# A two-layer decoder trunk on one core: VectorE's top-k in written order, four more tiles split on GpSimd, one weight load earlier

## The chip, the core and the metric

One Trainium2 chip, one of its cores. The metric is the device time of one execution in microseconds (us), median of the runs; lower is better. Engines: PE (TensorE matmul; PEld is its weight load), DVE (VectorE), ACT (ScalarE), POOL (GpSimd), SP (the queue that issues most DMAs).

## What is computed

Two layers over 256 tokens of width 1024. Each layer mixes the tokens (a gated linear recurrence beside sparse attention) and then runs an expert-retrieval mixer. The change lies almost wholly in the second half, which is, per layer:

```
q  = x @ wq                                  # 8 heads, 2 x 128 each
s  = einsum('thcd,ckd->thck', q, subkeys)    # two lists of 128 scores per head
sv, si = top_k(s, 16)
cand   = sv[:, :, 0, :, None] + sv[:, :, 1, None, :]
cv, ci = top_k(cand, 16)                     # 16 experts of 16384 per head
experts = ea * 128 + eb                      # ea, eb read from si at ci
gate    = softmax(cv)
y = sum over experts of  gelu(x . u_tab[e]) * gate * v_tab[e]
x = layer_norm(ALPHA * x + y)
```

## The kernel before

The expert tables are not gathered. All 128 tiles of `u_tab` (128 experts each) are multiplied with x, then weighted by a gate that is zero for unchosen experts, then all tiles of `v_tab` are multiplied. So TensorE has a fixed amount of dense work per layer, and the top-k (VectorE) runs beside the first half of it.

**A tile.** `wtile` loads 128x1024 numbers of 4 bytes by DMA into `raw`. ScalarE rounds them to `hi` (L103), and VectorE or GpSimd forms `lo = raw - hi` (L104). TensorE then does 24 matmuls per tile (`col_mm`, L112: 8 chunks, each as hi*hi, lo of x * hi, hi * lo of the weight). There are 4 buffers of `raw`, 3 of `hi`, 3 of `lo`, taken in the order of the tiles: the `hi` and `lo` of a tile can be written only when TensorE is done with the tile three places ahead.

**The top-k zone.** `query(h)` makes the query of head h: heads 4 to 7 need two tiles of `wq` each, whose `lo` is VectorE's. `top(h)` multiplies it with the subkeys (L798, 8 short matmul records), ScalarE copies the scores out of PSUM into `ss` (L800, two buffers), and `best16` finds the 16 best of each of four lists of 128 in five VectorE instructions: the best 8 (MAX8), their places (FIND_INDEX8), a copy without them (MATCH_REPLACE8), the next 8, their places (L785 to L789). FIND_INDEX8 and MATCH_REPLACE8 each have a short MATCH_VALUE_LOAD in front. `pairs(g)` adds the lists of four heads (L812, L816, nine instructions into `cd`) and runs eight `best16` over 50 candidates; `choices(g)` decodes the indices; `turn_round` transposes the result. Heads 2, 0, 1, 3 come first, then `pairs(0)`, heads 4 to 7, `pairs(1)`, `choices`.

**What sets the order.** `work()` is a generator that yields a cost after each piece; the loop below it emits tiles of `u_tab` whenever the costs have used up the `room`. The `lo` of tiles 0 to NPOOL-1 (14) goes to GpSimd. The emitted order isn't the order of an engine: the framework's scheduler reorders each engine's instructions. VectorE waits for its own earlier result through a semaphore.

**Layer 1's start.** `ORDER[1]` lists the steps of the mixing half; `d0` to `d5` are loads of constants, `d1` the weights `lw` of the recurrence's gates (L670), which the matmuls of L370 read.

Of the kernel before, what the change touches and what calls it, by code (L numbers as in the profile page):

```python
# [20 lines left out]
D = 1024  # L21
S = 256
# [24 lines left out]
NHF = 2  # L47
ROOT_ACT = {1, 2, 3}
NACT = 4
NPOOL = 14  # L50
NLATE = 4
NCAND = 50
CNT = [16 // (i + 1) for i in range(16)]
# [24 lines left out]
def trunk_kernel(ctx: ExitStack, tc: tile.TileContext, x, xt, cst, lam, pvec, brow, w_in, w_lx, w_v, w_q4, lru_w,  # L78
# [13 lines left out]
    def bank():  # L92
        return psp.tile([128, 512], F32, tag="ps", name="ps")


    def wtile(src, shape, lo_eng, dst=None):
        n = int(np.prod(shape))
        raw = ring.tile([128, 1024], F32, tag="raw", name="raw", bufs=4)
        if dst is None:
            dst = (ring.tile([128, 1024], F32R, tag="hi", name="hi"), ring.tile([128, 1024], F32R, tag="lo", name="lo"))  # L100
        nc.sync.dma_start(raw[:, :n], src)
        hi, lo, raw = dst[0][:, :n], dst[1][:, :n], raw[:, :n]
        ACT.copy(hi, raw)  # L103
        lo_eng.tensor_tensor(lo, raw, hi, op=ALU.subtract)  # L104
        if len(shape) == 2:
            hi = hi.rearrange("p (a b) -> p a b", a=shape[0])
            lo = lo.rearrange("p (a b) -> p a b", a=shape[0])
        return hi, lo
# [5 lines left out]
    def col_mm(ps, w, xT, t=ALL):  # L114
        for c in range(NCH):
            mm3(ps, (w[0][:, c, :], w[1][:, c, :]), (xT[0][:, c, t], xT[1][:, c, t]), c == 0, c == NCH - 1)
# [13 lines left out]
    def rtile(src, shape):  # L130
        raw = ring.tile([128, 1024], F32, tag="raw", name="raw", bufs=4)
        raw = raw[:, :shape[0] * shape[1]].rearrange("p (a b) -> p a b", a=shape[0])
        nc.sync.dma_start(raw, src)
        return raw
# [91 lines left out]
    for c0, c1 in ((0, 1), (1, 2), (2, 4), (4, 6), (6, 8)):  # L226
        s = slice(c0, c1)
        nc.sync.dma_start(xTf[:, s], xt[:, s])
        w = rtile(w_lx[0, :, s], (c1 - c0, 512))
# [36 lines left out]
    for l in range(NL):  # L266
# [3 lines left out]
        with tc.tile_pool(name="mix", bufs=1, reuse_waits="tile") as mp, \  # L270
# [433 lines left out]
            if l == 0:  # L704
                nc.sync.dma_start(lm, lam)
                psv = [bank(), bank()]
                for c0, c1 in ((0, 3), (3, 6), (6, 8)):
                    w = rtile(w_v[l, :, c0:c1], (c1 - c0, 280))
# [19 lines left out]
        with tc.tile_pool(name="peer", bufs=1, reuse_waits="tile") as pp:  # L728
# [7 lines left out]
            def act_tile():  # L736
                return pp.tile([128, 2, S], F32, name="act", bufs=NACT)

            def u_tile(a):
                if a % 2 == 0:  # L740
                    ub[a] = bank()
                ps = ub[a - a % 2]
                col_mm(ps[:, HALF[a % 2]], wtile(u_tab[l, a], (8, 128), POOL if a < NPOOL else DVE), xT)
                if a % 2:
                    at = act_tile()
                    ACT.activation(at.rearrange("p a b -> p (a b)"), ps, AF.Gelu_apprx_tanh)  # L746
                    kept[a - 1] = spill.tile([128, 2, S], F32, name="kept%d" % (a - 1), bufs=1)
                    ACT.dma_start(kept[a - 1], at)

            with tc.tile_pool(name="topk", bufs=1, reuse_waits="tile") as tk:  # L750
# [17 lines left out]
                def query(h):  # L768
                    qh = tk.tile([128, 2, S], F32, name="qh", bufs=2)
                    if h < 2:  # L770
                        for tb in range(2):
                            ACT.copy(qh[:, :, TB[tb]], qT4[tb][:, 2 * h:2 * h + 2])
                    else:
                        ps = bank()
                        for c in range(2):
                            k = 2 * h + c - 4
                            if "w%d" % k in W:
                                raw_mm(ps[:, c * 256:c * 256 + 256], W["w%d" % k])
                            else:
                                col_mm(ps[:, c * 256:c * 256 + 256], wtile(wq[l, k], (8, 128), POOL if h < 4 else DVE), xT)  # L780
                        ACT.copy(qh.rearrange("p a b -> p (a b)"), ps)
                    qhs[h] = qh

                def best16(v, ix, src, tmp):
                    DVE.max(v[:, 0:8], src)  # L785
                    DVE.max_index(ix[:, 0:8], v[:, 0:8], src)  # L786
                    DVE.match_replace(tmp, v[:, 0:8], src, -3e38)  # L787
                    DVE.max(v[:, 8:16], tmp)
                    DVE.max_index(ix[:, 8:16], v[:, 8:16], tmp)  # L789

                def top(h):

                    qh = qhs.pop(h)
                    ps = bank()
                    for tb in range(2):
                        for c in range(2):
                            k = tb * 2 + c
                            PE.matmul(ps[:, k * 128:k * 128 + 128], qh[:, c, TB[tb]], skt[:, c], start=True, stop=True)  # L798
                    ss = tk.tile([128, 4, 128], F32, name="ss", bufs=2)
                    ACT.copy(ss.rearrange("p a b -> p (a b)"), ps)  # L800
                    s2 = tk.tile([128, 4, 128], F32, name="s2", bufs=2)
                    for tb in range(2):
                        for c in range(2):
                            k, j = tb * 2 + c, tb * 4 + h % 4
                            best16(sv[:, h // 4, j, c], si[:, h // 4, j, c], ss[:, k], s2[:, k])
                            yield 1.45

                def pairs(g):

                    a, b = sv[:, g, :, 0], sv[:, g, :, 1]  # L810
                    for i in range(8):
                        DVE.tensor_tensor(cd[:, :, OFF[i]:OFF[i] + CNT[i]], a[:, :, i:i + 1].to_broadcast([128, 8, CNT[i]]),  # L812
                                          b[:, :, :CNT[i]], op=ALU.add)
                        if i % 4 == 3:
                            yield 1.2
                    DVE.tensor_tensor(cd[:, :, OFF[8]:NCAND], a[:, :, 8:16],  # L816
                                      b[:, :, 0:1].to_broadcast([128, 8, 8]), op=ALU.add)
                    for j in range(8):
                        best16(cv[:, g, j], ci[:, g, j], cd[:, j], c2[:, j])
                        yield 1.05  # L820
# [55 lines left out]
                    yield 1.8  # L876

                def turn_round():
                    for w in range(3):
                        ps = bank()  # L880
                        for tb in range(2):
                            src = ev[:, w, tb] if w < 2 else gate[:, tb]
                            PE.transpose(ps[:, TB[tb]], src.rearrange("p g k -> p (g k)"), ident)
                        tok = ps[:, :256].rearrange("p (q i) -> p q i", i=2)
                        if w < 2:
                            DVE.tensor_copy(eT[:, :, w], tok)
                        else:
                            DVE.tensor_scalar(gT[:, :, 0], tok, GSC, None, op0=ALU.mult)
                            DVE.scalar_tensor_tensor(gT[:, :, 1], tok, GSC, gT[:, :, 0], op0=ALU.mult, op1=ALU.subtract)
                        yield 0.5  # L890

                def work():
                    for h in (2, 0, 1, 3):
                        yield from top(h)
                    yield from pairs(0)
                    query(4)
                    yield 2.44 - 5.76
                    for h in range(4, 8):
                        if h < 7:
                            query(h + 1)  # L900
                            yield 2.44 - 5.76
                        yield from top(h)
                    yield from pairs(1)
                    yield from choices(0)
                    yield from choices(1)
                    yield 1.0
                    yield from turn_round()
                    yield 4.0

                for h in (2, 0, 1, 3):  # L910
                    if h == 0:
                        q_rows(1)
                    query(h)
                a, room = 0, 0.0
                for cost in work():
                    room -= cost
                    while room < 0 and a < 96:
                        u_tile(a)
                        room += 2.88 if a < NPOOL else 1.66
                        a += 1  # L920

            with tc.tile_pool(name="dense", bufs=1, reuse_waits="tile") as dp:

# [145 lines left out]
                for j, p in enumerate(body):  # L1069
# [11 lines left out]
                    if left <= 14 and pre:  # L1081
                        f, i = pre.pop(0)
                        f(i)
                        if left <= len(pre):
                            f, i = pre.pop(0)
# [194 lines left out]
```

## Time and profile before

| | us |
|---|---|
| three runs | 1940.72, 1940.97, 1942.93; median 1940.97 |
| the profiled execution, its own time | 1938.31 |
| its span, first to last instruction | 1936.5 |
| mean granted TensorE clock | 0.991 of full |

The span is what the views divide; 1.8 us of the execution lie around it, and the profiled execution is 2.7 us under the median. Times in the views count from the span's start. In layer 0 the top-k zone lies at about 160 to 340 us, in layer 1 at about 1124 to 1304. A busy PE isn't PE at its peak: starts of matmuls per microsecond tell more than the busy share.

### The profile page before, as it was taken

What the parts mean: (1) busy time and instruction counts of PE and PEld (TensorE: products, weight loads), DVE (VectorE), ACT (ScalarE), POOL (GpSimd) and SP (SyncE); (2) the same over time, 40 slices, a digit from 0 to 9 for tenths busy, and PEclk for the clock granted to TensorE, in tenths of its full rate; (3) what the DMA queues carried; (4) which work ended last, traced back from release to release, by engine and by line L of the source; (5) the groups of instructions that cost most, each with busy time, mean ns of one, the idle gap of its engine ahead of it and who ended that gap; (6) DMA issues with size and microseconds to landing.
All of it is one profiled execution on the core that took longest, in us unless ns stands there. A gap on an engine that the chain in (4) does not pass through costs nothing.

```text
span 1936.5 us, 32461 instructions
## 1 busy us (share of the span) xinstructions
PE 1894.0 (98%) x12580; PEld 1679.2 (87%) x12580; DVE 1330.6 (69%) x2553; ACT 966.3 (50%) x1579; POOL 83.1 (4%) x55
## 2 busy tenths in 40 slices
PE   8999899999999999999999998999999999999998
PEld 7858899999999888888777498999999998888886
DVE  5763994766666776767657549946666656777776
ACT  3635444555555555556445344444555555555553
POOL 0005200000000000000000062000000000000000
PEclk9999999999999999999999999999999999999999
DMA  7505557666667777888362054576666677778783
GB/s 267 175 1 172 153 191 236 211 207 192 204 203 242 244 241 240 282 283 300 140 227 66 0 187 154 189 236 212 196 203 201 201 245 240 244 243 286 250 265 106
DMA packets 130095, 393.91 MB, mean 203 GB/s; under 512 B 15634, under 2 KB 16404, under 8 KB 129812
## 3 DMA queue, kind: packets, MB, share of 16 engines
q1 hardware_dynamic: 111508, 358.28, 57.8%
q10 hardware_dynamic: 18432, 33.56, 4.7%
q8 instruction: 98, 1.61, 0.3%
q14 instruction: 57, 0.47, 0.1%
HBM read 357.18 MB, written 34.60 MB: 202 GB/s over the span
## 4 chain that ended last, share of the span: by engine, by line
PE 88%; DVE 8%; DMA 2%; issue 1%; ACT 1%; SPq 0%; POOL 0%; DVEq 0%; ACTq 0%; POOLq 0%
PE ps L112 39%; PE ps L995 34%; PE ps L954 3%; PE ps L119 3%; PE ps L590 3%; DVE lo L104 1%; PE ps L562 1%; DMA raw<-in_v_tab_dram 1%; PE ps L515 1%; DVE si L789 1%; DVE cd L812 1%; PE ps L232 1%; DVE s L787 1%; DVE si L786 0%; DVE t L866 0%
## 5 line engine op out<-in xcount | busy, mean ns | idle before, releaser
L104 DVE TENSOR_TENSOR lo<-raw,hi 128x1024 fp32r<-128x1024 f32 x516 | 635.1, 1232 | 396.4 <-ACT hi L103 396.0
L103 ACT CAST hi<-raw 128x1024 fp32r<-128x1024 f32 x548 | 575.1, 1050 | 663.4 <-PE ps L112 412.0
L112 PE MATMUL ps<-xThi,lo 128*128 128x256 f32 x2400 | 685.4, 286 | 20.0 <-DVE lo L104 19.7
L112 PE MATMUL ps<-xThi,hi 128*128 128x256 f32 x2400 | 693.5, 289 | 0.0
L112 PE MATMUL ps<-xTlo,hi 128*128 128x256 f32 x2400 | 684.0, 285 | 0.0
L995 PE MATMUL ps<-hi,W 128*128 128x512 f32 x1936 | 517.8, 389 | 0.0
L112 PEld LDWEIGHTS ps<-xThi,lo 128*128 128x128 f32 x2400 | 465.4, 194 | 21.9 <-DVE lo L104 21.2
L112 PEld LDWEIGHTS ps<-xThi,hi 128*128 128x128 f32 x2400 | 465.7, 194 | 0.9 <-issue 0.4
L112 PEld LDWEIGHTS ps<-xTlo,hi 128*128 128x128 f32 x2400 | 465.8, 194 | 0.3
L995 PEld LDWEIGHTS ps<-hi,W 128*128 128x128 f32 x1936 | 363.2, 188 | 75.4
L995 PE MATMUL ps<-lo,W 128*128 128x512 f32 x968 | 298.1, 389 | 0.2 <-DVE lo L104 0.2
L995 PEld LDWEIGHTS ps<-lo,W 128*128 128x128 f32 x968 | 181.6, 188 | 38.2 <-DVE lo L104 0.6
L986 ACT CAST W<-act 128x256 fp32r<-128x256 f32 x242 | 96.1, 402 | 94.6 <-PE ps L995 90.4
L987 DVE TENSOR_TENSOR W<-act,W 128x256 fp32r<-128x256 f32 x242 | 100.0, 422 | 9.5
L104 POOL TENSOR_TENSOR lo<-raw,hi 128x1024 fp32r<-128x1024 f32 x32 | 79.6, 2493 | 355.9 <-ACT hi L103 355.6
L972 DVE TENSOR_TENSOR act<-act,G 128x512 f32<-128x512 f32 x128 | 87.5, 685 | 6.6 <-DMA act<-kept 6.6
L958 ACT ACTIVATE G<-ps 128x256 f32<-128x256 f32 x256 | 81.2, 383 | 5.3
L943 DVE TENSOR_TENSOR ohg<-ohg,gT 128x2048 f16<-128x2048 f16 x64 | 78.2, 1225 | 2.0
L939 DVE TENSOR_TENSOR ohg<-iota,eT 128x2048 f16<-128x2048 f16 x64 | 77.9, 1220 | 0.0
L746 ACT ACTIVATE act<-ps 128x512 f32<-128x512 f32 x128 | 75.7, 591 | 0.1
L954 PE MATMUL ps<-ohg 128*128 128x128 f16 x1024 | 69.9, 219 | 0.0
L954 PEld LDWEIGHTS <-ohg 128*128 128x128 f16 x1024 | 58.8, 97 | 2.8
(256 smaller groups left out, 1179.6 us busy)
## 6 DMA issues: line engine op xcount, KB each, us to landing
raw<-in_u_tab_dram SPq DMA_DIRECT2D x256, 512.0 KB, 3.6
raw<-in_v_tab_dram SPq DMA_DIRECT2D x256, 512.0 KB, 4.2
kept<-act ACTq DMA_DIRECT2D x128, 256.0 KB, 2.5
act<-kept SPq DMA_DIRECT2D x128, 256.0 KB, 4.1
raw<-in_w_in_dram SPq DMA_DIRECT2D x24, 512.0 KB, 4.5
raw<-in_wq_dram SPq DMA_DIRECT2D x24, 512.0 KB, 3.6
ow<-in_w_out_dram SPq DMA_DIRECT2D x16, 512.0 KB, 7.8
qf<-in_w_q_dram SPq DMA_DIRECT2D x8, 512.0 KB, 3.8
```

Of the source, the lines that this page charges most:

```text
L103: ACT.copy(hi, raw)
L104: lo_eng.tensor_tensor(lo, raw, hi, op=ALU.subtract)
L112: PE.matmul(ps, a[m], b[n], start=start and i == 0, stop=stop and i == 2)
L746: ACT.activation(at.rearrange("p a b -> p (a b)"), ps, AF.Gelu_apprx_tanh)
L939: DVE.tensor_tensor(oh.rearrange("p q w a i -> p (q w) a i"), iota.unsqueeze(1).to_broadcast([128, 8, 128, 2]), eT[:, qs].rearrange("p q w ...
L943: DVE.tensor_tensor(og, oh[:, :, 0:1].to_broadcast([128, 4, 2, 128, 2]), gT[:, qs].unsqueeze(3).to_broadcast([128, 4, 2, 128, 2]), op=ALU. ...
L954: PE.matmul(ps[:, k * 128:k * 128 + 128], oh[:, q, 1, :, i], og[:, q, w, :, i], start=w == 0, stop=w == 1)
L958: ACT.activation(G[g][:, :, t1:t1 + 4], ps.rearrange("p (t g a) -> p g a t", g=2, a=64)[:, g], AF.Copy, scale=1.0 / GSC)
L972: i = DVE.tensor_tensor(act[a0], act[a0], G[a0 // 64][:, a0 % 64:a0 % 64 + 2, :], op=ALU.mult)
L986: ACT.copy(whi, at[:, a % 2])
L987: DVE.tensor_tensor(wlo, at[:, a % 2], whi, op=ALU.subtract)
L995: PE.matmul(accs[tb * 2 + hf], ww[m][:, TB[tb]], v[n][:, hf * 512:hf * 512 + 512], start=a == first[0] and (m, n) == (0, 0), stop=a == 127 ...
```

## The change

Five edits in the top-k zone and one in layer 1's list of steps:

- VectorE's instructions of the zone keep the order in which they are written (`manual_schedule`); the other engines are scheduled as before.
- `scores_of(h)` is taken out of `top(h)` and called ahead of the lists that need it; `query(4)` comes ahead of `top(3)`, and each later query ahead of the lists of the head before.
- NPOOL is 18 and not 14: four more `lo` per layer on GpSimd.
- The budget starts at -6.0 (two tiles more are written ahead of the first lists), and a tile of VectorE's counts 1.55 and not 1.66.
- `turn_round` does its three transposes first, then lets tiles pass, then copies.
- In layer 1, `d1` stands right behind `d0`.

```diff
-         "c0 I1 I0 d0 d4 P c1 V0 d2 V2 V1 d3 V3 d1 G0 d5 G3 G1 T g1 b0 g0 b1 g2 h0 g3 G2 q2 h1 D S q3 q1 kv q0 "
+         "c0 I1 I0 d0 d1 d4 P c1 V0 d2 V2 V1 d3 V3 G0 d5 G3 G1 T g1 b0 g0 b1 g2 h0 g3 G2 q2 h1 D S q3 q1 kv q0 "
...
-NPOOL = 14
+NPOOL = 18
...
-                def top(h):
-
+                sss = {}
+
+                def scores_of(h):
                     qh = qhs.pop(h)
...
+                    sss[h] = ss
+
+                def top(h, k0=0, k1=4):
+
+                    ss = sss[h]
                     s2 = tk.tile([128, 4, 128], F32, name="s2", bufs=2)
-                    for tb in range(2):
+                    for tb in range(k0 // 2, k1 // 2):
...
                 def work():
-                    for h in (2, 0, 1, 3):
-                        yield from top(h)
-                    yield from pairs(0)
+                    scores_of(2)
+                    scores_of(0)
+                    yield from top(2)
+                    scores_of(1)
+                    yield from top(0)
+                    scores_of(3)
+                    yield from top(1)
                     query(4)
                     yield 2.44 - 5.76
+                    yield from top(3)
+                    yield from pairs(0)
+                    scores_of(4)
                     for h in range(4, 8):
                         if h < 7:
                             query(h + 1)
                             yield 2.44 - 5.76
-                        yield from top(h)
+                        yield from top(h, 0, 2)
+                        if h < 7:
+                            scores_of(h + 1)
+                        yield from top(h, 2, 4)
                     yield from pairs(1)
                     yield from choices(0)
                     yield from choices(1)
-                    yield 1.0
                     yield from turn_round()
                     yield 4.0
...
-                a, room = 0, 0.0
-                for cost in work():
-                    room -= cost
-                    while room < 0 and a < 96:
-                        u_tile(a)
-                        room += 2.88 if a < NPOOL else 1.66
-                        a += 1
+                a, room = 0, -6.0
+                with tc.manual_schedule(engines={mybir.EngineType.DVE}):
+                    for cost in work():
+                        room -= cost
+                        while room < 0 and a < 96:
+                            u_tile(a)
+                            room += 2.88 if a < NPOOL else 1.55
+                            a += 1
```

Where the instructions move. First VectorE at the first lists of layer 0; `sv` are values, `si` places, `s_1471` the copy without the best eight. Before:

```order
L785 MAX sv<-ss 128x8 x2
L786 MAX_INDEX si<-sv,ss 128x8
L787 MATCH_REPLACE s_1471<-sv,ss 128x128
L786 MAX_INDEX si<-sv,ss 128x8
L788 MAX sv<-s_1471 128x8
L787 MATCH_REPLACE s_1471<-sv,ss 128x128
L789 MAX_INDEX si<-sv,s_1471 128x8
```

Now:

```order
L785 MAX sv<-ss 128x8
L786 MAX_INDEX si<-sv,ss 128x8
L787 MATCH_REPLACE s_1480<-sv,ss 128x128
L788 MAX sv<-s_1480 128x8
L789 MAX_INDEX si<-sv,s_1480 128x8
L785 MAX sv<-ss 128x8
L786 MAX_INDEX si<-sv,ss 128x8
```

Before, two lists alternate; now a list is finished before the next begins, and each instruction but MATCH_REPLACE and the first MAX reads what the one in front wrote.

Second, SP's loads of layer 0's zone, the order in which tiles pass through the buffers. Before:

```order
L752 DMA skt<-in_sk_dram 128x256
L101 DMA raw<-in_wq_dram 128x1024 x2
L101 DMA raw<-in_u_tab_dram 128x1024 x12
L101 DMA raw<-in_wq_dram 128x1024 x6
L101 DMA raw<-in_u_tab_dram 128x1024
L101 DMA raw<-in_wq_dram 128x1024 x2
L101 DMA raw<-in_u_tab_dram 128x1024 x115
```

Now:

```order
L101 DMA raw<-in_wq_dram 128x1024 x2
L101 DMA raw<-in_u_tab_dram 128x1024 x9
L101 DMA raw<-in_wq_dram 128x1024 x2
L101 DMA raw<-in_u_tab_dram 128x1024 x4
L101 DMA raw<-in_wq_dram 128x1024 x2
L101 DMA raw<-in_u_tab_dram 128x1024
L101 DMA raw<-in_wq_dram 128x1024 x2
L101 DMA raw<-in_u_tab_dram 128x1024
L101 DMA raw<-in_wq_dram 128x1024 x2
L101 DMA raw<-in_u_tab_dram 128x1024 x113
```

The six query tiles that came in one row behind u-tile 11 now come in pairs: behind u-tiles 8, 12, 13 and 14. With NPOOL at 18, all u-tiles up to 17 are GpSimd's.

Third, VectorE around the second pair of query tiles (`lo` of `query(5)`), behind the last list of `pairs(0)`. Now:

```order
L785 MAX cv<-cd 128x8
L786 MAX_INDEX ci<-cv,cd 128x8
L787 MATCH_REPLACE c_1366<-cv,cd 128x50
L788 MAX cv<-c_1366 128x8
L789 MAX_INDEX ci<-cv,c_1366 128x8
L104 TENSOR_TENSOR lo<-raw,hi 128x1024 x2
L785 MAX sv<-ss 128x8
```

All of `pairs(0)` stands between the `lo` of `query(4)` and these two; the four lists of head 3 stand ahead of `pairs(0)`.

## Rows read from the trace of the kernel before

**Rows 1.** The page's first part: busy time by engine

```profile
PE 1894.0 (98%) x12580; PEld 1679.2 (87%) x12580; DVE 1330.6 (69%) x2553; ACT 966.3 (50%) x1579; POOL 83.1 (4%) x55
```

**Rows 2.** Busy time in a stretch: us, PE, PEld, DVE, ACT, POOL, clock, DMA

```profile
200.00:262.00 62.00, 53.11 (x416) 52.50 (x415) 61.97 (x252) 25.59 (x32) 8.79 (x3) 0.94 0.47 145
```

**Rows 3.** The chain that ended last, both zones and layer 1's start: start, us, what

```profile
170.52 8.63 PE ps L112 x72
...
192.44 0.91 PE ps L798 x8
...
340.54 0.66 PE ps L883 x6
...
358.47 0.94 PE ps L954 x16
...
990.39 6.86 DMA lw<-in_lru_w_dram
...
1156.19 0.91 PE ps L798 x8
...
1323.37 0.94 PE ps L954 x16
```

**Rows 4.** Busy time by stretches of 4 us, layer 0, columns as in rows 2

```profile
208.00:212.00 4.00, 1.31 (x6) 1.31 (x7) 3.97 (x25) 0.62 (x2) 0.00 (x0) 0.82 0.09 11
212.00:216.00 4.00, 4.00 (x28) 4.00 (x28) 4.00 (x4) 3.55 (x4) 0.00 (x0) 0.76 0.45 141
```

**Rows 5.** VectorE in order of time: start, us, instruction, out<-in

```profile
187.35 0.49 DVE L785 MAX8 sv<-ss 128x8 f32<-128x128 f32 x2 [1.12 <-ACT ss L800]
...
191.12 0.29 DVE L789 FIND_INDEX8 si<-sv,s 128x8 uint32<-128x128 f32 x1
191.33 0.08 DVE L787 MATCH_VALUE_LOAD s<-sv,ss 128x8 f32 x1
191.38 0.28 DVE L787 MATCH_REPLACE8 s<-sv,ss 128x128 f32<-128x128 f32 x1
191.70 0.30 DVE L788 MAX8 sv<-s 128x8 f32<-128x128 f32 x1
192.03 0.09 DVE L789 MATCH_VALUE_LOAD si<-sv,s 128x8 f32 x1
```

**Rows 6.** VectorE by line: the same MAX8 over 50 candidates; busy, mean ns, idle

```profile
L788 DVE MAX8 cv<-c 128x8 f32<-128x50 f32 x32 | 6.6, 207 | 0.0
```

**Rows 7.** VectorE and GpSimd in order of time, where both add or subtract

```profile
200.18 2.40 POOL L104 TENSOR_TENSOR lo<-raw,hi 128x1024 fp32r<-128x1024 f32 x1 [0.48 <-ACT hi L103]
200.30 2.88 DVE L812 TENSOR_TENSOR cd<-sv 128x128 f32<-128x128 f32 x6
...
235.15 3.54 POOL L104 TENSOR_TENSOR lo<-raw,hi 128x1024 fp32r<-128x1024 f32 x1 [7.55 <-ACT hi L103]
...
236.55 3.22 DVE L104 TENSOR_TENSOR lo<-raw,hi 128x1024 fp32r<-128x1024 f32 x1
...
259.35 0.73 DVE L812 TENSOR_TENSOR cd<-sv 128x128 f32<-128x128 f32 x6
...
261.26 1.23 DVE L104 TENSOR_TENSOR lo<-raw,hi 128x1024 fp32r<-128x1024 f32 x1
```

**Rows 8.** ScalarE in order of time, layer 0's zone; idle time and releaser in brackets

```profile
171.14 0.61 ACT L800 COPY ss<-ps 128x512 f32<-128x512 f32 x1
...
186.73 0.59 ACT L800 COPY ss<-ps 128x512 f32<-128x512 f32 x1
...
196.17 1.05 ACT L103 CAST hi<-raw 128x1024 fp32r<-128x1024 f32 x1 [2.21 <-PE ps L112]
```

**Rows 9.** SP's queue, VectorE and PE in order of time, layer 1's start

```profile
987.90 0.48 SPq L674 DMA_DIRECT2D cw<-in_cmp_w_dram  x1
...
996.87 2.36 DVE L104 TENSOR_TENSOR lo<-raw,hi 128x1024 fp32r<-128x1024 f32 x2
...
997.39 2.83 PE L370 MATMUL ps<-xc,lw 128*128 128x256 f32 x12 [3.15 <-DMA lw<-in_lru_w_dram]
```

More of the change, by code (lines that the diff above doesn't have):

```diff
@@ L878, in turn_round @@
                 def turn_round():
+                    turned = []
                     for w in range(3):
@@ L883, in turn_round @@
                             PE.transpose(ps[:, TB[tb]], src.rearrange("p g k -> p (g k)"), ident)
-                        tok = ps[:, :256].rearrange("p (q i) -> p q i", i=2)
+                        turned.append(ps[:, :256].rearrange("p (q i) -> p q i", i=2))
+                    yield 5.0
+                    for w, tok in enumerate(turned):
                         if w < 2:
```

## The prediction

> **What bounds the kernel now.** I began with the page's busy time: PE is busy for 1894.0 us of the span and no other engine for more than 70% [rows 1]. So only time in which TensorE stands still, or runs at a low clock, can be won. The busy time by stretches shows where that is: between 200 and 262 us of layer 0 TensorE is busy for 53.1 of 62 us and VectorE for all of it [rows 2]. There VectorE is the bound; TensorE waits for its `lo`.
>
> The chain of waits gives the size. Undisturbed, 72 matmuls take 8.63 us [rows 3], so a tile (24) takes 2.88. From the scores of head 3 (192.44) to the first gate matmul (358.47) are 166.0 us [rows 3]; in them lie 51 tiles by TensorE's order (146.7 us), five score groups of 0.9 and the transposes (0.7), together 151.9. So 14.1 us are lost in layer 0 and, by the same sum from 1156.19 to 1323.37 [rows 3], 15.3 in layer 1: **29.4 us** in all. Of layer 0's 14.1, 8.9 are idle (62 less 53.1 [rows 2]). The other 5.2 are a low clock after idle time: the granted clock falls to 0.82 and 0.76 around a stall [rows 4]. Over three stalls that makes 1.7 us each beside the stall itself.
>
> **What an instruction of VectorE costs in the new order.** Where MAX8 follows the MATCH_REPLACE8 whose result it reads, it starts 0.32 us behind it, and MATCH_VALUE_LOAD starts 0.33 behind MAX8; an instruction that needs nothing of the one in front starts 0.21 behind it [rows 5]. Behind a value load, the replacement starts after 0.05; I take 0.07 for the searches. One `best16` in written order is then MAX 0.33, load 0.07, find 0.21, load 0.05, replace 0.32, MAX 0.33, load 0.07, find 0.21, which makes 1.59 us. Alternating it is 1.24: head 1's four lists run from 187.35 to 192.3, a search behind the value load of 192.03 [rows 5]. Over 50 candidates each of the five is 0.08 shorter (207 ns [rows 6] against 0.28 to 0.30 [rows 5]): 1.19. For 32 and 16 of them per layer that is some 17 us more VectorE per layer; four `lo` moved away give back 4.9 (1.23 each [rows 7]). It costs the kernel something only where TensorE catches up with VectorE.
>
> The Trainium skill's page VectorE: DVE Perf Modes, section The DRAIN you can't avoid, says otherwise: the next instruction waits for the pipe in any case, and a semaphore between two costs nothing extra. The trace differs, 0.32 against 0.21 [rows 5]; I take the trace. By the page's rule the sum would be the second rival's.
>
> **What GpSimd costs VectorE.** Additions and subtractions of the two engines exclude each other. A `lo` of VectorE alone takes 1.23, but 3.22 beside one of GpSimd's; six additions take 0.73 alone, but 2.88 when they meet a `lo` of GpSimd's that began 0.12 before [rows 7]. Searches aren't slowed. GpSimd needs 2.40 per `lo` [rows 7] of TensorE's 2.88, so VectorE finds gaps of 0.5.
>
> **Layer 0's zone, step by step in the new order.** A tile's `hi` follows TensorE by 1.1 us [rows 8], and its `lo` buffer comes free when the tile three ahead is done.
> - Heads 2 and 0: scores at 171.75 [rows 8], eight lists, done at 184.5. Head 1's scores come at 187.3 as before [rows 8] (the same tiles lie ahead of them): done at 193.7.
> - `lo` of `query(4)`: the first by 195.0, the second only once u-tile 7 is done (196.2) and rounded (197.3 [rows 8]): done at 198.5. VectorE stands still for 2.3 us here, with head 3 queued behind; TensorE wants these tiles at 199 and 202, so nothing is lost yet.
> - Head 3 until 204.9. Then nine additions of `pairs(0)` meet GpSimd, whose `lo` begin at about 203.2, 206.1, 208.9: some four fit the gap at 205.6, the rest the one at 208.5. Done at 209.0.
> - Eight `best16` until 218.5. TensorE wants the first tile of `query(5)` at 217.3 (193.35, eight tiles, scores of head 4). GpSimd begins `lo` of u-tile 13 at 217.5, so VectorE gets the port at 219.9, done at 221.1: **stall of 3.8**, and 1.7 of low clock. Between the bounds 0 (all additions in one gap) and 6.3 (one missed gap more) I take 3.8, since the sum lies 1 us on that side.
> - `query(6)` and `query(7)` are in time: VectorE is through with them at about 231 and 240, GpSimd starts its next `lo` after (231.7, 242), TensorE wants them at 230.6 to 233.5 and 241.
> - Scores of head 6 stand right behind the query's last matmul and wait for its copy out of PSUM, 0.6 [rows 8]: **0.7**.
> - u-tile 18, the first that VectorE makes: after the scores of head 7 TensorE has 2.5 tiles (7.1 us); VectorE has the copy 0.6, four lists 6.4, additions 1.1, `lo` 1.2, together 9.3: **stall of 2.2**. u-tile 19 (two short `best16` and a `lo`, 3.7 against 2.88): **0.8**. Low clock again 1.7, bounds 0 and 3.4.
> - From there the decoding has about 1.7 us of work per `lo`, 2.85 with it against 2.88: nothing. ScalarE's exponential waits for VectorE, but the `hi` behind it are wanted later still: nothing. With `turn_round`'s copies five tiles later, TensorE has tiles: nothing. The onehot stage has fewer tiles left for VectorE: nothing.
>
> Lost after: 3.8 + 1.7 + 0.7 + 2.2 + 0.8 + 1.7 = 10.9 per layer. Layer 1 has the same order: 21.8. Gain 29.4 - 21.8 = **7.6 us**.
>
> **Layer 1's gate weights.** PE waits 3.15 us for `lw` [rows 9], which is issued last of four and takes 6.86 [rows 3]. Now it takes the place at 987.90 [rows 9]; even with 6.86 it lands at 994.8, and the gate matmuls end at 997.6. The tile behind them needs a `lo` that is ready at 998.1 (996.87 and 1.23 [rows 9, 7]), against 1000.22 now (997.39 and 2.83 [rows 9]): **2.1 us**, bounds 0 (another wait takes it) and 3.15. The loads that it passes feed matmuls 10 us later: nothing.
>
> **Sum.** The profiled execution took 1938.3 (span and 1.8): less 9.7 makes 1928.6. It lies 2.7 under the median, so I say **1931** for the median.
>
> **The rivals.**
> - *The additions get through in one gap.* Then `query(5)` is in time at 217.3, and 5.5 per layer are saved more: 1931 less 11, **1920**. For it: a lead of 2.4 us decides, and small errors add up over 48 `best16`. Against it: the gap is 0.5 us for 1.1 us of additions.
> - *Waiting for one's own result costs nothing.* Lists cost 1.24 and 0.79 as when alternating: `query(5)` is in time, u-tile 18 is late by 0.8 only, and the loss is 1.5 to 3.2 per layer: 25 to 28 us less, **1914**. Against it: the pairs of rows 5, few but clear.
> - *Slower: GpSimd's extra tiles block VectorE's `lo` at every query.* Of `query(6)`, the second `lo` ends 0.6 us ahead of GpSimd's u-tile 14; if VectorE comes more than that later, it waits 2.4 and TensorE 1.8 and 1.7 of clock; the same again at `query(7)`, and at `pairs(0)` a third gap (2.4). That makes 9.4 per layer more, 18.8: **1950**. It decides only from a lateness that the sum doesn't show.
> - *The stalls only move.* With the low clock at its upper bounds (1.7 more at each of the two stalls) a layer loses 14.3: gain 0.8 and at most 2.1 for `lw`, **1938**.
>
> **How the numbers follow.** About 0.2% (3.9 us) is what a measurement can tell from no change: faster is under 1937, slower over 1945. Forecast 0.50; additions in one gap 0.20; no price of waiting 0.12; stalls only move 0.11; slower 0.07. The first three are faster, with a little taken off the forecast's upper end: 0.79; same 0.14; slower 0.07. The range holds the first three cases and most of the fourth, 1914 to 1940.
>
> **What would show it.** Right: in both zones a stall near 217 to 221 at the first tile of `query(5)`, with a `lo` of VectorE of about 3 us or one starting where GpSimd's ends; a second at u-tile 18; VectorE's lists 1.6 us each; from head 3's scores to the first gate matmul some 177 us (56 tiles by the new order, 161.1, with scores and transposes 166.3, and 10.9 lost); no wait for `lw`. Wrong: lists at 1.24 each, TensorE without a stall in the query stretch, or stalls at `query(6)` and `query(7)` with a clock under 0.9 throughout.

## The result and the profile after

The changed kernel takes **1929.85 us** (five runs, 1924.85 to 1932.1) against 1940.97 for the kernel before: ratio 0.9939, interval 0.9922 to 0.9956. It is faster by 11.1 us, 1.2 under the forecast of 1931. Measured again later (below), the ratio was 0.9938 [0.9921, 0.9954]. The profiled execution took 1932.1, its span 1930.3.

The page's first part, and of its fifth the group in which TensorE waits for a `lo` (busy us, mean ns, idle us before it and what ended most of that):

```profile
PE 1892.3 (98%) x12577; PEld 1675.0 (87%) x12580; DVE 1344.8 (70%) x2545; ACT 967.1 (50%) x1579; POOL 99.6 (5%) x63
...
L112 PE MATMUL ps<-xThi,lo 128*128 128x256 f32 x2400 | 682.8, 285 | 12.3 <-DVE lo L104 12.0
```

Against [rows 1], VectorE is busy for 14 us more, GpSimd for 16 more. TensorE's idle time ahead of this group was 20.0 on the page of before:

```profile
L112 PE MATMUL ps<-xThi,lo 128*128 128x256 f32 x2400 | 685.4, 286 | 20.0 <-DVE lo L104 19.7
```

The chain that ended last, as in [rows 3]; both zones:

```profile
191.97 0.89 PE ps L799 x8
...
220.46 8.65 PE ps L112 x59
...
237.21 1.04 ACT hi L103
...
238.25 0.49 ACT qh L781
...
238.79 1.16 PE ps L799 x8
...
260.36 79.28 PE ps L112 x646
...
369.08 0.94 PE ps L973 x16
...
1154.30 0.89 PE ps L799 x8
...
1331.52 0.94 PE ps L973 x16
```

From head 3's scores to the first gate matmul are 177.1 us in layer 0 and 177.2 in layer 1, where the new order's work takes 166.3: 10.8 and 10.9 lost, forecast 10.9. Three waits start the long runs of matmuls at 220.46, 238.79 and 260.36: `query(5)`, the scores of head 6, u-tile 18. TensorE in order of time, with the idle time before and its releaser:

```profile
220.46 0.58 PE L112 MATMUL ps<-xThi,lo 128*128 128x256 f32 x1 [3.43 <-DVE lo L104]
...
238.79 1.05 PE L799 MATMUL ps<-skt,qh 128*128 128x128 f32 x7 [1.50 <-ACT qh L781]
...
260.36 0.39 PE L112 MATMUL ps<-xThi,lo 128*128 128x256 f32 x1 [1.80 <-DVE lo L104]
```

What holds the first one, from the timelines of GpSimd and of VectorE (head 1's lists, the additions of `pairs(0)`, the last search there and the two `lo` behind it):

```profile
202.54 2.41 POOL L104 TENSOR_TENSOR lo<-raw,hi 128x1024 fp32r<-128x1024 f32 x1 [0.43 <-ACT hi L103]
205.42 2.59 POOL L104 TENSOR_TENSOR lo<-raw,hi 128x1024 fp32r<-128x1024 f32 x1 [0.47 <-ACT hi L103]
...
216.98 2.34 POOL L104 TENSOR_TENSOR lo<-raw,hi 128x1024 fp32r<-128x1024 f32 x1 [6.23 <-ACT hi L103]
```

```profile
186.87 0.30 DVE L785 MAX8 sv<-ss 128x8 f32<-128x128 f32 x1 [2.79 <-ACT ss L801]
...
188.46 0.28 DVE L785 MAX8 sv<-ss 128x8 f32<-128x128 f32 x1
...
190.03 0.28 DVE L785 MAX8 sv<-ss 128x8 f32<-128x128 f32 x1
...
204.21 3.83 DVE L818 TENSOR_TENSOR cd<-sv 128x128 f32<-128x128 f32 x8
...
217.41 0.20 DVE L789 FIND_INDEX8 ci<-cv,c 128x8 uint32<-128x50 f32 x1
217.53 4.01 DVE L104 TENSOR_TENSOR lo<-raw,hi 128x1024 fp32r<-128x1024 f32 x2
```

A list over 128 scores starts 1.59 and 1.57 us after the one in front; the additions take 3.8 us, as they meet two `lo` of GpSimd's (they begin 0.74 us before the one of 202.54 ends; seven of them come through, the eighth waits for the one of 205.42); the two `lo` that TensorE waits for take 4.01 and not 2.4, behind GpSimd's of 216.98.

Where the clock falls (us, PE, PEld, DVE, ACT, POOL, granted clock):

```profile
216.00:220.00 4.00, 1.02 (x10) 0.82 (x8) 3.86 (x12) 1.41 (x2) 2.34 (x1) 1.00 0.02 7
220.00:224.00 4.00, 3.54 (x18) 3.55 (x19) 3.83 (x16) 0.00 (x0) 0.00 (x0) 0.57 0.51 184
...
256.00:260.00 4.00, 2.56 (x22) 2.35 (x20) 3.84 (x20) 1.99 (x3) 0.00 (x0) 1.00 0.00 2
260.00:264.00 4.00, 3.64 (x19) 3.64 (x20) 3.76 (x20) 0.00 (x0) 0.00 (x0) 0.62 0.56 193
```

It falls to its lower level (1.2 GHz) behind a stall, as in [rows 4]: 18 matmul records between 220 and 224 where an undisturbed stretch has 34 to 36.

Layer 1's start, TensorE in order of time, and two rows of the chain, some 20 and 30 us on:

```profile
994.52 1.99 PE L370 MATMUL ps<-xc,lw 128*128 128x256 f32 x8 [0.70 <-DVE xc L364]
```

```profile
1017.58 5.95 PE ps L112 x48
...
1025.48 7.45 PE ps L112 x48
```

The wait for `lw` [rows 9] is gone. The 48 matmuls at 1025 take 7.45 us instead of an undisturbed 5.95: a low clock that this kernel has here in some executions and not in others (the second profile, run 10, has 5.95).

The two profiled executions differ by 6.2 us (1938.3 to 1932.1), the medians by 11.1. The zone gives 7.7 and the wait for `lw` 2.4; against that, this execution has a second low clock at 1042 (1.7) that the one before lacks, and between 899 and 913 TensorE waits 2.1 us for tiles of `v_tab` where it waited 0.2 before. The second profile has no low clock at 1042 and 0.7 of such waits.

### The profile page after: what moved, and what is told of

Same layout as the page of the kernel before. It is cut to its first block, busy times and chain, and to the rows that moved or that the text cites. A ratio compares the mean times of both kernels' runs of the same rounds, so it can differ in the third digit from the quotient of the medians.

```text
span 1930.3 us, 32458 instructions
## 1 busy us (share of the span) xinstructions
PE 1892.3 (98%) x12577; PEld 1675.0 (87%) x12580; DVE 1344.8 (70%) x2545; ACT 967.1 (50%) x1579; POOL 99.6 (5%) x63
## 4 chain that ended last, share of the span: by engine, by line
PE 91%; DVE 5%; DMA 2%; ACT 1%; issue 1%; POOL 0%; SPq 0%; DVEq 0%; ACTq 0%; POOLq 0%
PE ps L112 42%; PE ps L1014 34%; PE ps L973 3%; PE ps L590 3%; PE ps L119 3%; DMA raw<-in_v_tab_dram 1%; PE ps L562 1%; DVE lo L104 1%; PE ps L515 1%; PE ps L799 1%; PE ps L232 1%; DVE cd L818 0%; ACT hi L103 0%; PE ps L542 0%; PE ps L438 0%
## 5 line engine op out<-in xcount | busy, mean ns | idle before, releaser
L104 DVE TENSOR_TENSOR lo<-raw,hi 128x1024 fp32r<-128x1024 f32 x508 | 623.9, 1230 | 360.4 <-ACT hi L103 360.1
L112 PE MATMUL ps<-xThi,lo 128*128 128x256 f32 x2400 | 682.8, 285 | 12.3 <-DVE lo L104 12.0
L112 PE MATMUL ps<-xThi,hi 128*128 128x256 f32 x2400 | 690.8, 288 | 0.0
L112 PE MATMUL ps<-xTlo,hi 128*128 128x256 f32 x2400 | 682.4, 284 | 0.0
L112 PEld LDWEIGHTS ps<-xThi,lo 128*128 128x128 f32 x2400 | 463.3, 193 | 14.0 <-DVE lo L104 13.1
L112 PEld LDWEIGHTS ps<-xThi,hi 128*128 128x128 f32 x2400 | 463.5, 193 | 1.2 <-issue 0.4
L112 PEld LDWEIGHTS ps<-xTlo,hi 128*128 128x128 f32 x2400 | 463.8, 193 | 0.2
L104 POOL TENSOR_TENSOR lo<-raw,hi 128x1024 fp32r<-128x1024 f32 x40 | 96.1, 2406 | 365.9 <-ACT hi L103 365.8
```

What stands on the lines that cost most here:

```text
L112: PE.matmul(ps, a[m], b[n], start=start and i == 0, stop=stop and i == 2)
```

## The experiments

All ratios are to the kernel before, in runs on the same chip; a ratio of 0.001 is 1.9 us. Beside the profile, each run lists its mean granted clock: span times what the clock lacks of 1 is what an execution lost to the low clock, 16.4 us on average over 15 runs of the kernel before (mean clock 0.9915), and about 11 in the changed one (0.994). A small part of that (some 3 to 4 us in the profiles) lies behind the last matmul and costs nothing.

**1. The gate weights' load alone.**

```diff
-         "c0 I1 I0 d0 d4 P c1 V0 d2 V2 V1 d3 V3 d1 G0 d5 G3 G1 T g1 b0 g0 b1 g2 h0 g3 G2 q2 h1 D S q3 q1 kv q0 "
+         "c0 I1 I0 d0 d1 d4 P c1 V0 d2 V2 V1 d3 V3 G0 d5 G3 G1 T g1 b0 g0 b1 g2 h0 g3 G2 q2 h1 D S q3 q1 kv q0 "
```

> The kernel before with the gate weights' load of layer 1 issued first, and nothing else of the change. Theory from the changed kernel's trace: PE's first gate matmul no longer waits for lw (3.15 us before, 0.70 after, ended by VectorE), but the waits that follow give most of it back, since 2.4 us of lead at the start of the gates' matmuls had shrunk to 0.7 about 110 us later: 0.7 us faster than before, within 0 to 1.5. Rival, the prediction's own term: the lead is kept, 2.1 us faster (1938.9 against 1941).

1934.59 (11 runs) against 1939.99 (15 runs): ratio 0.9971 [0.9962, 0.9980], **5.6 us faster**. Both expectations are missed, from above. In the two profiles the stretch from layer 0's last expert matmul to the first matmul of L438 (some 10 us behind the gates) takes 44.3 us for 46.7, and the one from there to the first matmul of L139 (queries that are loaded unsplit, ahead of the zone) 107.8 for 109.3: 2.4 of wait, and 1.5 of a low clock that is missing here. By the clocks of all runs this kernel loses 12.5 us to it against 16.4, so the low clock makes most of the difference. My reading of 0.7 came from the one profile of the changed kernel, in which the low clock at 1042 had eaten 1.7 of it (the one at 1025 is no loss against the profile of before, which has it too, at 1029).

**2. Two lists alternating** in VectorE's written order.

```diff
-                        for c in range(2):
-                            k, j = tb * 2 + c, tb * 4 + h % 4
-                            best16(sv[:, h // 4, j, c], si[:, h // 4, j, c], ss[:, k], s2[:, k])
-                            yield 1.45
+                        j = tb * 4 + h % 4
+                        best16x2([(sv[:, h // 4, j, c], si[:, h // 4, j, c], ss[:, tb * 2 + c], s2[:, tb * 2 + c])
+                                  for c in range(2)])
+                        yield 1.45
+                        yield 1.45
```

(`best16x2` issues each of the five steps for both lists; the search and the copy of one list stay together. `pairs` likewise.)

> The changed kernel, with the instructions of two lists of 16 alternating in VectorE's written order, so that hardly one reads the result of the one in front. Theory (a list costs more when each of its instructions waits for its own predecessor): 1.24 us per list over 128 scores instead of 1.57, and about 0.8 over 50 candidates instead of 1.165; pairs(0) is done 3 us earlier, so the two lo of query(5) lie ahead of GpSimd's and TensorE's stall of 4.0 us there is gone with its low clock, and that at u-tile 18 falls from about 2.2 to 0.9. Of 10.9 us lost per layer from head 3's scores to the first gate matmul 2.5 to 4 remain: 1914 to 1917 us, 13 to 16 less than the changed kernel. Rival 1 (waiting for one's own result costs nothing): lists stay at 1.57 and the time at 1930. Rival 2 (lists get cheaper, but TensorE stands for GpSimd's exclusion and the scores, not for the lists): stall near 217 to 220 stays over 2 us, 1925 to 1930.

1912.99, ratio 0.9862 [0.9847, 0.9877]: 14.9 us under the changed kernel by the ratios, as expected. VectorE in order of time: two lists take 2.36 us, 1.18 each.

```profile
188.03 0.49 DVE L793 MAX8 sv<-ss 128x8 f32<-128x128 f32 x2 [6.06 <-ACT ss L812]
...
190.39 0.47 DVE L793 MAX8 sv<-ss 128x8 f32<-128x128 f32 x2
```

The chain runs through `query(5)` without a break, and the page's idle time ahead of L112 is down from 12.3:

```profile
194.02 23.03 PE ps L112 x192
...
254.91 77.88 PE ps L112 x646
```

```profile
L112 PE MATMUL ps<-xThi,lo 128*128 128x256 f32 x2400 | 680.4, 284 | 2.2 <-DVE lo L104 1.8
```

TensorE's order of tiles is the same as in the changed kernel, and the additions of `pairs(0)` took longer here (5.6 us for 4.0), so the gain comes from the lists. Waiting for one's own result has a price here, and TensorE pays it. Rivals 1 and 2 fall.

**3. U-tile 13's `lo` on VectorE.**

```diff
-                col_mm(ps[:, HALF[a % 2]], wtile(u_tab[l, a], (8, 128), POOL if a < NPOOL else DVE), xT)
+                col_mm(ps[:, HALF[a % 2]], wtile(u_tab[l, a], (8, 128), POOL if a < NPOOL and a != 13 else DVE), xT)
```

> The changed kernel, with the lo of u-tile 13 made by VectorE instead of GpSimd, in VectorE's order three lists behind the lo of query(5). Theory (the two engines' subtractions exclude each other, and this lo of GpSimd's is what holds query(5)): VectorE's two lo at 217.5 us take 2.45 us instead of 4.01, the stall falls from 4.0 to about 2.4; u-tile 13 itself comes up to 1 us late: 1 to 2 us less per layer, 1926 to 1928 us. Rival (no exclusion there; the two lo are long for another reason): they take about 4 us again, and the 1.2 us more work on VectorE make it 0 to 3 us slower, 1930 to 1933.

1922.9, ratio 0.9921 [0.9908, 0.9935]. The chain: the two `lo` of `query(5)` take 2.34 us, and u-tile 13, which is now late itself, starts TensorE again at 225.13.

```profile
216.89 2.34 DVE lo L104 x2
...
223.95 1.14 DVE lo L104
...
225.13 1.57 PE ps L112 x11
```

So VectorE's two `lo` were long because of GpSimd's. TensorE's wait at `query(5)` falls from 3.43 to 1.78 in both layers; u-tile 13 takes 0.96 of that back in layer 0 and nothing in layer 1. No low clock followed in layer 0. The gain over the changed kernel is 3.5 us by the ratios, with intervals that overlap (7 by the medians).

**4. Fourteen tiles on GpSimd.**

```diff
-NPOOL = 18
+NPOOL = 14
```

> The changed kernel with fourteen tiles of lo on GpSimd as before, instead of eighteen. VectorE makes u-tiles 14 to 17, one between every one or two lists of heads 6 and 7. Theory (VectorE is the bound from 217 to 262 us, but idles 5.7 us between 230 and 250 us of the changed kernel's profile): of 4.9 us more work per layer about 2 us fall on TensorE: 1932 to 1938 us. Rival 1: the idle time covers all of it and no lo meets GpSimd's, 1930 or a little less. Rival 2 (the eighteen tiles carry the whole gain): back to 1939 to 1941.

1916.51, ratio 0.9887 [0.9871, 0.9903]: **10 us faster** than the changed kernel, where the expectations had it slower, equal or a little less. In the chain the last piece ahead of the transposes begins right behind head 7's scores:

```profile
252.46 1.11 PE ps L799 x8
253.57 96.36 PE ps L112 x803
```

No stall at u-tile 18. The number stands in two places: it names the engine, and it sets the budget (2.88 us of VectorE's work per tile below NPOOL, 1.55 from there). The next two runs take them apart.

**5. The engine alone, and the budget alone.**

```diff
-                col_mm(ps[:, HALF[a % 2]], wtile(u_tab[l, a], (8, 128), POOL if a < NPOOL else DVE), xT)
+                col_mm(ps[:, HALF[a % 2]], wtile(u_tab[l, a], (8, 128), POOL if a < 14 else DVE), xT)
```

> The changed kernel with the lo of u-tiles 14 to 17 on VectorE, but each of these tiles still placed after 2.88 us of VectorE's work, as the budget for GpSimd's tiles has it. It takes apart the kernel with fourteen tiles, which was 11 us faster than the changed one and differs in the engine and in the budget (1.55 us instead of 2.88 for these four). Theory 1, the budget made that gain (TensorE gets four more tiles ahead of the gates, and its stall at u-tile 18 of 2.1 us and the low clock behind it go): nothing of it here; VectorE has 4.9 us more work per layer, of which some 1 to 2.5 us lengthen the stall at u-tile 18: 1931 to 1935 us. Theory 2, GpSimd's lo cost the time by keeping VectorE from its additions and subtractions: most of the gain is here, 1917 to 1924.

```diff
-                            room += 2.88 if a < NPOOL else 1.55
+                            room += 2.88 if a < 14 else 1.55
```

> The changed kernel with GpSimd still making eighteen tiles, but u-tiles 14 to 17 placed after 1.55 us of VectorE's work each, as if VectorE made them. Theory 1 (the budget): TensorE's stall at u-tile 18 is gone with its low clock, the stalls at query(5) and at the scores of head 6 stay: 1914 to 1920 us. Theory 2 (GpSimd's lo block VectorE): 1927 to 1931, as the changed kernel.

Engine alone: 1931.84, ratio 0.9951 [0.9932, 0.9969], no faster than the changed kernel. Budget alone: 1919.23, ratio 0.9885 [0.9866, 0.9905], the whole gain. Theory 1 holds. With the smaller budget TensorE's order has 33.5 tiles behind head 7's scores and ahead of the transposes instead of 29.5: four that would have come beside the gates, where TensorE never waits in any of these profiles. The page of the engine alone, then of the budget alone:

```profile
L112 PE MATMUL ps<-xThi,lo 128*128 128x256 f32 x2400 | 683.1, 285 | 13.1 <-DVE lo L104 12.9
```

```profile
L112 PE MATMUL ps<-xThi,lo 128*128 128x256 f32 x2400 | 682.2, 284 | 8.5 <-DVE lo L104 8.2
```

The trace shows only a part of the 10 us. In the profile of the budget alone (its slowest execution, 1923.77) the two zones lose 7.3 and 8.4 instead of 10.8 and 10.9: 6.0 less, 3.6 of it the wait at u-tile 18 and 1.7 the low clock behind it in layer 0. In layer 1 the low clock took 3.4 us, as in the changed kernel, all of it now behind `query(5)`.

As an engine, GpSimd's four more tiles are worth nothing that these runs can tell apart (0.9951 against 0.9939, 0.9887 against 0.9885); as a budget they cost the changed kernel 10 us.

**6. The written order taken away**, everything else as changed.

```diff
-                with tc.manual_schedule(engines={mybir.EngineType.DVE}):
+                if True:
```

> The changed kernel without the written order: VectorE's instructions in the zone stand as the scheduler places them. It lets lists alternate (1.24 us each), and it pulls eight products and sums of the first half's decoding (2.3 us for the comparison, 1.2 for each product, 0.5 for a sum, by the changed kernel's trace) ahead of the lo of query(5). Theory 1 (VectorE's place in the order decides there): TensorE's stall at query(5) grows from 4.0 to 6 to 9 us, that at u-tile 18 (2.1) goes: between 1928 and 1936 us, about as the changed kernel. Theory 2 (the written order itself is what gained): 1936 to 1941, as before. Theory 3 (alternation is all that counts): 1913 to 1918.

1935.29 (12 runs), ratio 0.9981 [0.9971, 0.9991]: the written order is worth 8 us of the change. The time lies inside theory 1's range, but not through its place. ScalarE in order of time:

```profile
205.18 1.28 ACT L841 ACT_TABLE_LOAD   x1
211.82 0.31 ACT L841 ACTIVATE gt<-gt 128x128 f32<-128x128 f32 x1 [5.36 <-DVE gt L840]
212.15 1.28 ACT L746 ACT_TABLE_LOAD   x1
...
213.94 1.04 ACT L103 CAST hi<-raw 128x1024 fp32r<-128x1024 f32 x1
```

and TensorE:

```profile
215.03 0.38 PE L112 MATMUL ps<-xThi,hi 128*128 128x256 f32 x1 [2.69 <-ACT hi L103]
...
217.84 0.58 PE L112 MATMUL ps<-xThi,lo 128*128 128x256 f32 x1 [2.31 <-POOL lo L104]
```

With the decoding pulled ahead, the softmax's exponential stands early in ScalarE's queue, waits 5.36 us for VectorE, and every `hi` waits behind it. Then GpSimd's `lo` comes late too. (In the kernel before, whose order is also the scheduler's, this exponential waits 4.22 us, at 211.38.) Alternating lists, which this order has, don't make up for it. This kernel has every other edit of the change, and it lies 1.9 us over run 1, which has the load alone: without the written order the other edits gain nothing that shows. What they are worth one by one beside it, but for the budget, wasn't run.

**7. The gate weights' load undone in the changed kernel.** The diff of run 1, backwards.

> The changed kernel with the gate weights' load of layer 1 issued fourth again. Alone, the early load gave 5.6 us: 2.4 at its place in the profile, and the rest in less time at the low clock, whose cause is open. Theory 1 (2.4 of wait, and a low clock that the wait brings with it or makes likelier): PE waits about 3 us for lw again, the mean granted clock falls, 1933 to 1936 us. Theory 2 (the wait alone, the clock being chance): 1931 to 1933, clock as in the changed kernel (0.994).

1929.76 (7 runs), ratio 0.9953 [0.9936, 0.9970]: 2.7 us over the changed kernel by the ratios, with intervals that overlap. The wait is back (3.56 us for `lw`, and the clock at 0.79 behind it), yet layer 1's zone lost 5.1 us less in this profile. VectorE's additions, then GpSimd:

```profile
1167.12 1.59 DVE L818 TENSOR_TENSOR cd<-sv 128x128 f32<-128x128 f32 x8
1168.62 0.22 DVE L822 TENSOR_TENSOR cd<-sv 128x64 f32<-128x64 f32 x1
```

```profile
1165.45 2.41 POOL L104 TENSOR_TENSOR lo<-raw,hi 128x1024 fp32r<-128x1024 f32 x1 [0.44 <-ACT hi L103]
1168.33 2.77 POOL L104 TENSOR_TENSOR lo<-raw,hi 128x1024 fp32r<-128x1024 f32 x1 [0.47 <-ACT hi L103]
```

They began 0.74 us before GpSimd's `lo` ended (1167.86), went on into the next one, and made GpSimd wait: nine additions in 1.7 us, `query(5)` in time. That is the first rival of the prediction, in one layer of one execution. What decided it isn't shown: in the changed kernel the additions begin 0.74 us before the end as well (204.21 against 202.54 and 2.41), and there the eighth is caught.

**8. Scores of head 6 a tile later**, on top of run 2.

```diff
+                        if h == 5:
+                            yield 3.0
                         if h < 7:
                             scores_of(h + 1)
+                        if h == 5:
+                            yield -3.0
```

> The kernel with two lists alternating (1913.0 us), and the scores of head 6 one u-tile later on TensorE. Theory (of the 2 us that each layer still loses there, 1.5 are TensorE's wait for the copy of query(6)): the wait is gone, TensorE has no gap over 0.6 us between head 3's scores and the first gate matmul, 3 us less: 1910 us. Rival (VectorE gets head 6's scores later by a tile, and the lists behind them become the wait): 1912 to 1915.

**1910.3**, ratio 0.9851 [0.9833, 0.9869]: the fastest kernel here, 17 us under the changed one. TensorE has no gap over 0.6 us in either zone, and the profile's clock is 0.999 (its execution, 1905.5, is the fastest of the five). From the chain:

```profile
190.96 0.89 PE ps L810 x8
...
358.28 0.94 PE ps L990 x16
```

167.3 us for 166.3 of work.

**9. The load undone there:** the diff of run 7 on top of run 8.

> The fastest kernel so far (1910.3 us: two lists alternating, scores of head 6 a tile later) with the gate weights' load of layer 1 issued fourth again. Its zone has no gaps left, so the load's own worth shows with little else moving. Theory 1 (2.4 us of wait, and now and then a low clock behind it, 1.7): 1912 to 1915 us. Theory 2 (5.6 us, as for the early load alone in the kernel before): 1915 to 1917. Theory 3 (nothing, as it seemed when it was undone in the changed kernel): 1909 to 1911.

1914.93, ratio 0.9879 [0.9859, 0.9899]: 5.4 us slower by the ratios, 4.6 by the medians. That agrees with run 1; the interval of run 7's 2.7 has room for it too. TensorE, and the stretches around it:

```profile
985.53 4.51 PE L370 MATMUL ps<-xc,lw 128*128 128x256 f32 x12 [3.41 <-DMA lw<-in_lru_w_dram]
```

```profile
984.00:988.00 4.00, 2.46 (x7) 2.04 (x8) 3.12 (x7) 0.84 (x2) 0.00 (x0) 0.77 0.87 329
988.00:992.00 4.00, 4.00 (x24) 3.64 (x23) 0.00 (x0) 1.68 (x4) 0.00 (x0) 0.80 0.73 236
```

The stretch to L438 takes 48.7 us here against 44.3 in run 8: 2.7 of wait and 1.7 of low clock behind it. Another low clock at 1020 adds 1.5.

**10. The changed kernel once more.**

> The changed kernel once more, for a second profile and for its time beside the others of this call. Theory (its spread of 7 us comes from how often the clock falls after a gap, 1.7 us each, and from whether the additions of pairs(0) get through one gap of GpSimd's): net of the low clock the runs agree within some 4 us around 1918; the profile has stalls at query(5), the scores of head 6 and u-tile 18, each of them in both layers unless the additions get through at once; 1926 to 1932 us. Rival (the spread is something that the zone does not show): net times differ as much as the times.

1927.46, ratio 0.9938 [0.9921, 0.9954]. The three stalls are there in both layers, with 177.3 and 177.4 us from head 3's scores to the gates (the first profile: 177.1 and 177.2). Each run's time less its loss to the low clock lies between 1914 and 1918, 4 us wide where the times are 6 (1921.9 to 1927.9): the low clock looks like a part of the spread and not the whole of it, as far as clocks listed to 0.001 (1.9 us) can tell. No additions got through at once in this profile.

## Why the prediction was right

**The sum.** Forecast 1931, measured 1929.85, well inside the range. The stalls came at the places that the sum names, with VectorE's lists and the exclusion by GpSimd behind the first, and the zone's total is right to 0.1. So close a total is luck in part: the terms below are off by up to 0.8, and they cancel. The interval of the ratio puts the gain between 8.5 and 15 us, so 9.7 and 11.1 can't be told apart.

**The zone.** Gain forecast 7.6; measured 7.7 (29.4 less 10.8 and 10.9), 7.3 in the second profile. Found per layer: 3.4 + 1.7 + 1.5 + 1.8 + 1.7, and 0.7 because three groups of scores take 1.1 and not 0.9.

- *List prices.* 1.59 forecast, 1.57 found; 1.19 over 50 candidates, 1.165 found (from 208.21 to 217.53 for eight). Alternating, a list takes 1.18 (run 2), and the kernel 14.9 us less by the ratios. The Trainium skill's page VectorE: DVE Perf Modes, section The DRAIN you can't avoid, says that a semaphore between two instructions costs nothing extra, as measured there on copies. For these searches the runs differ, 1.57 against 1.18.
- *Query(5).* Stall forecast 3.8, found 3.4: seven additions came through the first gap and not four, and `pairs(0)` was done at 217.5, not 218.5. The cause is shown in two parts: with u-tile 13's `lo` elsewhere the two take 2.34 and the stall is 1.8 (run 3); with shorter lists there is none (run 2).
- *Scores of head 6.* Forecast 0.7, found 1.5. I had counted the copy out of PSUM (0.6; it took 0.49) behind the last matmul, but ScalarE was rounding a tile then: the chain has 1.04 us of `hi` ahead of the copy.
- *U-tile 18.* 2.2 + 0.8 + 1.7 forecast; found 1.8, no second one in this profile (0.4 in one layer of the second), and 1.7. The term was too large: two layers of it are 9.4, two layers found are 7. Run 5's budget, which removes this stall alone, gained 10 by the ratios, of which its trace places 6.0 in the zones.
- *Low clock.* 1.7 behind each of the two long stalls, as forecast. That it is one drop per stall doesn't always hold: layer 1 of the second profile has 3.4 behind `query(5)` and nothing behind u-tile 18.

**The gate weights' load** was mis-sized: 2.1 with an upper bound of 3.15. Runs 1 and 9 give 5.6 and 4.6 to 5.4. The wait itself gave 2.4 to 2.7, near the term; what the step left out is the low clock behind the wait (1.7 in run 9) and a further one, 30 us on, that came less often without it (1.5 in runs 1 and 9). The three profiles with the late load all have this further one; of the ten with the early load four have it, but three of these, the changed kernel's first among them, have a second at its heels (1.7), so the profiles don't show how much of it the load saves. I had priced the low clock behind the zone's stalls and not behind this one, because [rows 9] showed none there in that execution. 7.7 and 5.6 make 13.3 where 11.1 was measured; the interval (8.5 to 15) holds both. Run 7 gives the load only 2.7 in the changed kernel, with an interval that holds nothing as well as 5.6; in its profile layer 1 escapes the stall at `query(5)`, and that the load has to do with it isn't shown.

**The rivals.** *Additions in one gap* is real but rare: one of twelve layers in the six profiles that keep this stretch (run 7). In all twelve the additions begin 0.73 to 0.74 us before GpSimd's `lo` ends, so how early they began didn't decide it. *Waiting costs nothing* was wrong about the chip, but its 1914 is what alternating lists gave (1913). *Extra tiles block VectorE at every query* didn't come: `query(6)` and `query(7)` were in time. *The stalls only move* neither.

**What I didn't see.** "Four `lo` moved away give back 4.9" was charged to VectorE's load and no further. The tiles moved to GpSimd also moved in the budget, and that gave TensorE fewer tiles where it ran dry. The prediction had the stall at u-tile 18 from the right rows, the 2.5 tiles behind head 7's scores, and didn't ask what had put so few there.

## What to carry to other kernels

A constant that names an engine can also feed a planner's budget: undo each use apart before crediting the engine. In an order written by hand, let two independent chains alternate: here that was worth more than the whole change. Price a wait on TensorE together with the low clock that may follow, and take more than one profile before believing that the gain was given back.

## What the runs showed of the hardware

- MAX8, FIND_INDEX8 and MATCH_REPLACE8 over 128 scores: 1.57 us per list in dependent order, 1.18 with two lists alternating.
- VectorE's additions and GpSimd's `lo` exclude each other in both directions: in run 7 GpSimd's took 2.77, and the additions 1.59 instead of 3.83. Which of the two goes first isn't settled by their starts: from the same lead of 0.74 us the eighth addition was caught in eleven layers and none in the twelfth, and in layer 0 of run 8 nine additions that began 0.05 us behind a `lo` of GpSimd's (201.58, 201.53) ran through in 1.1 us while that `lo` took 3.46.
- The same wait of TensorE is followed by a low clock in one execution and not in another: behind `lw` the clock was 0.79 in run 7 and 0.77 in run 9, but no drop followed in the profile of before. A kernel without gaps lost least: run 8's profile has a mean clock of 0.999, the kernel before 0.991.
